# Earlier loads for W1 tiles in the steady blocks, and later sums of one W1 tile at the start, in a two-layer matmul with GELU

## The chip, the cores and the metric

The kernel runs on one core of one Trainium2 chip. The metric is the device time of one execution in microseconds (us), with the median of several executions quoted. A profiled execution also has a span, from its first to its last instruction, which is 1 to 2 us shorter than the time. The engines are called PE (TensorE), PEld (its weight loads), DVE (VectorE), ACT (ScalarE), POOL (GpSimd) and SP (SyncE, which here only issues DMA; SPq is its queue of instructions).

The Trainium skill, a set of notes on the chip, is cited by the title of the page and the section.

## The reference

```python
batch, m, k, h, n = 16, 512, 768, 3072, 768      # x, w1, b1, w2: normal draws, float32
y = np.matmul(x, w1) + b1
y = 0.5 * y * (1.0 + erf(y / np.sqrt(2.0)))
out = np.matmul(y, w2)
```

## The kernel before

The 8192 rows of x are worked in eight blocks of 1024. Both matmuls use a Strassen-like scheme: seven products of half-size operands in place of eight, paid for with sums and differences on DVE. W1 is cut into twelve tiles. A tile holds seven operands, made of its raw data by four sums on DVE (`prep_wt`), 672 KB in all in fp16. In the first two blocks, which are interleaved, each tile is loaded raw, gets its sums, and is stored in that form in device memory (`keep`). The six later blocks (the steady blocks) only read the stored tiles back (`load_wt`). In a steady block twelve units of the first matmul (`Unit1`, 4.53 us each) are followed by seven units of the second (`Unit3`).

PE runs the program of one unit (`i`) interleaved with the end of the unit before it (`j`). This is a cut from `period`; lines left out are marked with `...`, and the comments are mine:

```python
        def period(i, j, fill):
            ...
            if i:
                p1(i, 0, i.C)        # matmuls into bX
                copy_xy(i)           # ACT copies bX to bY
            ...
            if j:
                p7(j)                # matmuls into bY, then on DVE: c22 = bY + w
            fill(1)                  # sums on DVE, loads: fill(1) to fill(6)
            ...                      # p5(i): matmuls into bW, ACT copies them to w
            if j:
                p3(j)                # matmuls into bZ, then on DVE: c12 = bZ + w
            fill(3)
            if i:
                p6(i)                # matmuls into the bY that copy_xy filled
            if j:
                j.right_done()       # ACT: GELU of c12 and c22
            fill(4)
            if j:
                p4(j)                # matmuls into the bY that c22 was read from
            fill(5)
            if i:
                p2(i)
            fill(6)
```

`p6(i)` waits for ACT's `copy_xy(i)`. `p4(j)` adds to the same bank of bY from which DVE reads for c22, so it waits for that DVE add.

The homes of the tiles in steady blocks, and when they are asked for:

```python
    wt_late = [wt_at(o_wt2), wt_at(o_wt2 + WT_N)] + wt_own[:2]     # four homes
    ...
        def load_wt(n):
            hi = hi_of(n)
            if n >= NH:
                wts[n] = wt_late[n % 4]
                nc.sync.dma_start(out=wts[n], in_=w1s[hi][:])
                return
    ...
        def fill_mm1(sb, k, slot):
            ...
            if slot == 5:
                if k + 3 < NH and n + 3 not in wts:
                    load_wt(n + 3)
```

With four homes, tile k+3 goes where tile k-1 was, so SP waits until unit k-1 is finished. The next block's x tiles (POOL) and their transposes (SP) and the first ten W2 pieces (the "ring", SP) are asked for in the same units.

## Time and profile before

| | before |
|---|---|
| time, median of 6 runs | 854.43 us (853.19 to 855.50) |
| span of the profiled execution | 852.4 us |
| PE, DVE, ACT busy | 99%, 78%, 49% |
| start-to-start spacing of matmuls with 512, 384, 192 columns (medians) | 216, 162, 82 ns |
| all matmuls at their median spacing | 839.6 us |
| excess over that spacing, whole program | 7.8 us |

The spacing is the distance between the starts of successive matmuls in the timeline. "Excess" is the sum of what goes beyond the median spacing of the shape, and a "wait" of PE below is such an excess at one place. It is a little longer than the idle time that the profile prints in brackets, because the profile's matmul durations overlap.

From the page of the kernel before: busy time by engine, the chain of work that ended last by engine, and one group of matmuls (count, busy us, mean ns, idle us before them and what ended it):

```profile
PE 845.8 (99%) x6432; PEld 569.2 (67%) x6432; DVE 667.8 (78%) x1128; ACT 421.1 (49%) x686; POOL 83.3 (10%) x135
...
PE 93%; DMA 5%; ACT 1%; DVE 0%; issue 0%; POOL 0%; ACTq 0%
...
L383 PE MATMUL bX<-arena 128*128 128x512 f16 x564 | 138.6, 379 | 0.6 <-DMA arena<-w1s 0.5
```

The waits of PE, before (total us, times, longest us); those of L735 and bT lie in the first 14 us:

```profile
PE bX L735 <- DVE arena L721: 1.2, 1, 1.2
PE bX L383 <- DMA arena<-w1s: 0.5, 1, 0.5
PE bT L308 <- ACT arena L310: 0.4, 1, 0.4
PE bY L383 <- ACT bY L601: 0.4, 1, 0.4
PE bT L308 <- DVE arena L741: 0.2, 1, 0.2
```

Busy time says little about how full PE is ("Perfetto Trace Analysis", Identifying the Most-Contended Engine: matmuls are pipelined). The spacing says more. "TensorE: Matmul & The Clock Gate" (Wait — 56ns, not 53.3ns?) gives 215.7 ns for 512 columns at full clock, and this trace has 216. So PE is at its roof nearly everywhere, and a change of loads and sums can only win what stands in the few waits. Two places have waits that the change could touch.

The first is the second steady block. The chain of waits (start us, length us) names, apart from three x loads that are issued in the first 14 us, two loads in the whole program: one of a W1 tile at the start and one of a stored tile. The third line, from the timeline of PE, is the first use of that stored tile:

```profile
24.64 11.81 DMA arena<-in_w_dram
...
366.35 10.18 DMA arena<-w1s
```

```profile
376.58 0.82 PE L383 MATMUL bX<-arena 128*128 128x512 f16 x3 [0.55 <-DMA arena<-w1s]
```

Tile 10 was asked for at 366.35 us, landed at 376.53, and PE stood for 0.71 us.

The second place is at the start. This is the timeline of the kernel before from 33.8 to 48 us (start us, length us, engine, line, operation, tiles, in brackets the idle time before it and what ended it):

```profile
33.76 1.79 DVE L189 TENSOR_TENSOR arena<-arena 128x384 f16<-128x384 f16 x5
...
35.47 0.68 DVE L608 TENSOR_TENSOR arena<-bY,arena 128x512 f32<-128x512 f32 x1
...
36.47 1.14 DVE L189 TENSOR_TENSOR arena<-arena 128x384 f16<-128x384 f16 x3 [0.32 <-DMA arena<-in_w_dram]
37.53 0.68 DVE L636 TENSOR_TENSOR arena<-bZ,arena 128x512 f32<-128x512 f32 x1
...
38.24 1.15 ACT L399 ACTIVATE arena<-arena,b1t 128x1024 f16<-128x1024 f32 x1 [1.12 <-DVE arena L636]
...
41.13 0.60 ACT L601 COPY bY<-bX 128x512 f32<-128x512 f32 x1
...
41.78 1.46 PE L383 MATMUL bY<-arena 128*128 128x512 f16 x6 [0.38 <-ACT bY L601]
...
44.24 1.02 DVE L189 TENSOR_TENSOR arena<-arena 128x768 f16<-128x768 f16 x2
...
45.30 0.69 DVE L608 TENSOR_TENSOR arena<-bY,arena 128x512 f32<-128x512 f32 x1
...
46.40 1.46 PE L383 MATMUL bY<-arena 128*128 128x512 f16 x6
```

Read it downwards. Four of the five sums at 33.76 belong to W1 tile 1. The sums of tile 6 at 36.47 waited for the load of tile 6, which landed at 36.44. Behind them on DVE stands the c12 add (L636), behind that ACT's GELU (L399) and four more ACT operations without a pause, the last of them the copy that PE needs at 41.78. The c22 add (L608) ends at 45.99, and the second three of the six matmuls at 46.40 are p4, which needs it.

### The profile page before, as it was taken

Reading aid. Unit: us, or ns where it says so; the run is one execution under the profiler, and the core shown is the slowest. Engines: PE = TensorE matmul, PEld = TensorE weight load, DVE = VectorE, ACT = ScalarE, POOL = GpSimd, SP = SyncE. Lnnn points to the kernel's source line nnn. Section 1 sums busy time; section 2 is a strip of 40 time slices with the busy share of each in tenths; the row PEclk is TensorE's granted clock in tenths of the full one; section 3 lists DMA queues with packets and bytes.
Section 4 is the critical chain, followed back from the end, with each engine's and each line's share of the span. In section 5 each row is a group of like instructions: output and inputs, shape, how many; then the busy total and the mean of one; then the engine's idle time right before and its main releaser. Section 6 shows DMA issues by size and latency. Waiting matters only on the chain.

```text
span 852.4 us, 16481 instructions
## 1 busy us (share of the span) xinstructions
PE 845.8 (99%) x6432; PEld 569.2 (67%) x6432; DVE 667.8 (78%) x1128; ACT 421.1 (49%) x686; POOL 83.3 (10%) x135
## 2 busy tenths in 40 slices
PE   9999999999999999999999999999999999999998
PEld 5444445687544897448974499645995469944798
DVE  4956678786657998679976799667996689956998
ACT  4777762122277513774138722477216771267611
POOL 5021100002100002000020000200012000010000
PEclk9999999999999999999999999999999999999999
DMA  9995987649989698996989789896998969967398
GB/s 225 201 271 86 256 166 257 253 190 221 227 242 290 206 326 289 294 265 228 337 285 298 220 279 335 278 300 192 312 343 257 311 177 329 354 218 270 99 310 284
DMA packets 143522, 219.05 MB, mean 257 GB/s; under 512 B 61756, under 2 KB 84724, under 8 KB 143444
## 3 DMA queue, kind: packets, MB, share of 16 engines
q1 hardware_dynamic: 117968, 179.83, 66.0%
q0 software_dynamic: 25440, 38.15, 20.9%
q8 instruction: 50, 0.82, 0.4%
q14 instruction: 28, 0.23, 0.1%
q10 hardware_dynamic: 36, 0.01, 0.0%
HBM read 180.30 MB, written 47.87 MB: 268 GB/s over the span
## 4 chain that ended last, share of the span: by engine, by line
PE 93%; DMA 5%; ACT 1%; DVE 0%; issue 0%; POOL 0%; ACTq 0%
PE bY L383 20%; PE bY L488 15%; PE bX L383 13%; PE bX L488 10%; PE bZ L383 7%; PE bW L383 7%; PE bZ L488 5%; PE bW L488 5%; PE bY L427 5%; DMA arena<-in_x_dram 3%; PE bZ L427 2%; PE bW L427 2%; PE bX L427 2%; DMA arena<-in_w_dram 1%; DMA arena<-w1s 1%; PE bY L575 1%
## 5 line engine op out<-in xcount | busy, mean ns | idle before, releaser
L189 DVE TENSOR_TENSOR arena<-arena 128x1536 f16<-128x1536 f16 (+7 forms) x632 | 403.5, 669 | 6.0 <-PE bW L427 1.1
L383 PEld LDWEIGHTS <-arena 128*128 128x128 f16 x1974 | 192.4, 98 | 225.7 <-DMA arena<-w1s 1.8
L488 PEld LDWEIGHTS <-arena 128*128 128x128 f16 x3528 | 292.1, 98 | 8.4 <-issue 0.4
L383 PE MATMUL bY<-arena 128*128 128x512 f16 x846 | 214.4, 379 | 0.4 <-ACT bY L601 0.4
L608 DVE TENSOR_TENSOR arena<-bY,arena 128x512 f32<-128x512 f32 (+1 forms) x102 | 69.4, 681 | 126.7 <-PE bY L383 88.2
L383 PE MATMUL bX<-arena 128*128 128x512 f16 x564 | 138.6, 379 | 0.6 <-DMA arena<-w1s 0.5
L488 PE MATMUL bY<-arena 128*128 128x192 f16 x1500 | 138.3, 246 | 0.0
L601 ACT COPY bY<-bX 128x512 f32<-128x512 f32 (+1 forms) x143 | 78.6, 550 | 119.4 <-DVE arena L537 82.0
L399 ACT ACTIVATE arena<-arena,b1t 128x1024 f16<-128x1024 f32 x94 | 108.0, 1149 | 54.0 <-DVE arena L636 54.0
L621 ACT COPY arena<-bW 128x512 f32<-128x512 f32 (+1 forms) x147 | 81.0, 551 | 92.0 <-PE bW L488 43.9
L488 PE MATMUL bX<-arena 128*128 128x192 f16 x1020 | 93.1, 246 | 0.1
L636 DVE TENSOR_TENSOR arena<-bZ,arena 128x512 f32<-128x512 f32 (+1 forms) x102 | 69.3, 679 | 22.7 <-PE bZ L383 18.7
L383 PE MATMUL bZ<-arena 128*128 128x512 f16 x282 | 76.2, 379 | 0.0
L383 PE MATMUL bW<-arena 128*128 128x512 f16 x282 | 76.2, 379 | 0.0
L427 PEld LDWEIGHTS <-arena 128*128 128x128 f16 x528 | 51.6, 98 | 34.1 <-issue 0.2
L404 ACT ACTIVATE arena<-bX,b1t 128x512 f16<-128x512 f32 x94 | 64.0, 681 | 10.0 <-PE bX L383 10.0
L520 POOL DMA_DIRECT2D out_dram<-arena x42 | 30.5, 728 | 391.8 <-DVE arena L632 355.6
L404 ACT ACTIVATE arena<-bY,b1t 128x512 f16<-128x512 f32 x94 | 63.3, 674 | 0.0
L652 ACT COPY bZ<-bY 128x512 f32<-128x512 f32 (+1 forms) x54 | 29.0, 537 | 66.0 <-DVE arena L636 31.8
L294 POOL DMA_DIRECT2D arena<-in_x_dram x60 | 32.3, 544 | 265.0 <-DMA arena<-arena 154.6
L488 PE MATMUL bZ<-arena 128*128 128x192 f16 x504 | 48.5, 246 | 0.0
L488 PE MATMUL bW<-arena 128*128 128x192 f16 x504 | 48.5, 246 | 0.0
(60 smaller groups left out, 401.2 us busy)
## 6 DMA issues: line engine op xcount, KB each, us to landing
arena<-w2s SPq DMA_DIRECT2D x294, 288.0 KB, 4.6
arena<-w1s SPq DMA_DIRECT2D x72, 672.0 KB, 6.5
out_dram<-arena POOLq DMA_DIRECT2D x42, 384.0 KB, 4.7
w2s<-arena SPq DMA_DIRECT2D x49, 288.0 KB, 3.9
arena<-in_x_dram POOLq DMA_DIRECT2D x60, 192.0 KB, 6.8
w1s<-arena SPq DMA_DIRECT2D x12, 672.0 KB, 7.8
arena<-in_w_dram POOLq DMA_DIRECT2D x17, 384.0 KB, 7.2
out_dram<-arena SPq DMA_DIRECT2D x17, 384.0 KB, 3.5
```

What stands on the lines that cost most here:

```text
L189: nc.vector.tensor_tensor(out=o, in0=a, in1=b, op=op)
L294: nc.gpsimd.dma_start(out=xhs[t], in_=xr[:, sb * 8 + t, :])
L383: nc.tensor.matmul(out=dst[:, 0:RH], lhsT=w1_op(self.wt, slot)[:, c, :], rhs=a[:, c, :], start=first and c == 0, stop=c == self.C - 1, ski ...
L399: nc.scalar.activation(out=self.G[1][:, hi, :, :], in_=self.tmp, func=GELU, bias=b1t[:, 2 * hi + 1:2 * hi + 2])
L404: nc.scalar.activation(out=self.G[0][:, hi, row, :], in_=bank[:, 0:RH], func=GELU, bias=b1t[:, 2 * hi:2 * hi + 1])
L427: nc.tensor.matmul(out=dst[:, 0:N2], lhsT=a, rhs=w[:, :, c, :], start=first and c == 0, stop=c == self.C - 1, skip_group_check=True)
L488: nc.tensor.matmul(out=dst[:, t * N4:(t + 1) * N4], lhsT=a, rhs=w[:, c, :], start=first and c == 0 and t == ts[0], stop=c == NQ - 1, skip_ ...
L520: eng.dma_start(out=orr[:, s0:s0 + 2, right * N2:(right + 1) * N2], in_=self.dst[:, r].rearrange("p t h n -> p t (h n)"))
L601: nc.scalar.copy(out=bY[u.g % 2][:, 0:u.F], in_=bX[u.g % 2][:, 0:u.F])
L608: nc.vector.tensor_tensor(out=u.c22(), in0=bY[u.g % 2][:, 0:u.F], in1=w[:, 0:u.F], op=ADD)
L621: nc.scalar.copy(out=w[:, 0:u.F], in_=bW[:, 0:u.F])
L636: nc.vector.tensor_tensor(out=u.c12(), in0=bZ[:, 0:u.F], in1=w[:, 0:u.F], op=ADD)
```

## The change

Its intent, as far as the edit shows it: at the start, ask for the four sums of tile 1 two units later, and for the stores of the tiles in another order, with tile 1 behind tiles 2 to 6; in the steady blocks, give tiles 4, 5 and 6 homes of their own in the room of nested sums that are made only later, and ask for tiles 3 to 10 in the first five units.

```diff
+    wt_far = [wt_at(o_lev + 8 * RH + k * WT_N) for k in range(3)]
+    assert 8 * RH + 3 * WT_N <= 8 * LB
@@ load_wt
-                wts[n] = wt_late[n % 4]
+                sb, k = divmod(n, NH)
+                wts[n] = wt_far[k - 4] if 4 <= k < 7 else wt_late[(sb + 2 + k - 7 * (k > 6)) % 4]
@@ fill_a (the start), slot 4 and slot 5
-                if pos in (3, 4):
-                    prep_wt(pos - 3)
+                if pos in (3, 6):
+                    prep_wt(pos // 6)
...
-                if seq[pos][0] == 1:
-                    keep(seq[pos][1])
+                for n in {at[1, 0]: (0, 2, 3, 4, 6, 5), at[1, 1]: (1,)}.get(
+                        pos, seq[pos][1:] if pos > at[1, 6] and seq[pos][0] and seq[pos][1] > 6 else ()):
+                    keep(n)
@@ fill_mm1 (steady blocks), slot 5
-                if k + 3 < NH and n + 3 not in wts:
-                    load_wt(n + 3)
+                for m in {0: (3, 4), 1: (5, 6, 7), 2: (8,), 3: (9,), 4: (10,), 8: (11,)}.get(k, ()):
+                    if sb * NH + m not in wts:
+                        load_wt(sb * NH + m)
```

The added lines shift the line numbers: L383 becomes L386, L601 L604, L608 L611, L636 L639.

## The prediction

> **What bounds the kernel.** TensorE. The page shows PE busy 845.8 of 852.4 us (99%), DVE 78%, ACT 49%. Since the Trainium skill ("Perfetto Trace Analysis", Identifying the Most-Contended Engine) warns that matmul occupancy says little about the distance to the roof, I took the spacing of matmul starts in the timeline: 216 ns for 512 columns, 162 for 384, 82 for 192. "TensorE: Matmul & The Clock Gate" (Wait — 56ns, not 53.3ns?) states 215.7 ns for 512: the trace agrees, TensorE streams at full rate. All matmuls at these spacings make 839.6 us; 7.8 are excess. The change touches two places of it:
>
> - 41.78 us: 0.55, and 46.40: 0.08. PE waits for ACT's copy into bY.
> - 376.6 to 388.4 us, second steady block: 0.71 + 0.18 + 0.25 = 1.14. W1 tile 10, asked for at 366.35, landed at 376.53 (10.2 us; median 6.5), tile 11 at 381.25, each just late. In the chain of waits the other blocks repeat every 102.9 us, this one takes 104.1; 12 x 21 x 0.216 + 7 x 84 x 0.0825 = 102.9, so the others have nothing left.
>
> At most 1.8 us (0.2%) can be won.
>
> **What the change does.** Nothing is added or removed.
>
> (a) Steady blocks: tiles 4, 5, 6 get homes of their own. Tiles 7 to 10 are asked for three units (14 us) earlier. Between 353 and 367 us four W1 loads of 672 KB shrink to one, where x loads, transposes and ring loads share the DMA engines (one set for all issuers, skill "DMA: Bandwidth & Descriptors", Issuing engines are not separate DMA queues). Tile 11 keeps its place but meets less traffic. I expect all 1.14 us back, and no new wait from the early burst (tiles 4 to 6 near 330 us, used 10 us later or more).
>
> (b) Start: the four sums of tile 1 (0.39 us each) leave 34.0 to 35.6 us and come at about 45.2. This does not remove the 0.55 us: the next sums on DVE wait for tile 6's load, landed 36.44, which nothing moves (DVE already idled 0.32 us there). After it the DVE add at 37.5, the GELU at 38.24 and four more ACT operations in a row up to the copy ending 41.73 stay. But at 45.2 the sums' 1.5 us stand ahead of the bY add (L608), which then ends at about 47.3 instead of 45.99; the p4 matmuls into that bY started at 47.05. Estimate: 0.3 us of new wait. The stores' new order costs nothing: tile 1's store lands by about 54 us, the load over it is asked for at 55.9.
>
> **Sum.** 854.24 − 1.14 + 0.3 = 853.4 us; range 852.0 to 854.8. Faster by over 2%: 0.01; within 2%: 0.98; slower by over 2%: 0.01.
>
> **What would show it.** (a): no PE wait on w1s in the waits; steady blocks all near 102.9 us; landing of w1s under 10 us. (b): the gap near 41.8 us stays about 0.5 us, and one of about 0.3 appears before a bY matmul near 47, released by DVE L611 (the old L608).
>
> **What would make it wrong.** The stall at 376 us differs between executions, so the median holds less of it; tile 6 lands earlier, and (b) wins 0.5 instead; the early burst delays the first x loads, their transposes hold up SyncE's queue, and tile 11 is late in every block (5 x 0.5 us lost).

## The result, and the profile after

| | before | after |
|---|---|---|
| time, median of 6 runs | 854.43 us (853.19 to 855.50) | 853.25 us (853.03 to 854.13) |
| span of the profiled execution | 852.4 us | 851.5 us |

The ratio is 0.9988 with a 95% interval of 0.9975 to 1.0001. A ratio is the mean time of one kernel's fast runs over that of the other's of the same rounds, so it is not quite the ratio of the medians quoted. 853.25 lies in the range of 852.0 to 854.8. The interval just includes 1, so the times alone do not show a gain; what follows about tenths of a microsecond rests on the profiles.

The waits of PE, after. The wait on stored tiles is gone from the list (those of L738 and bT lie in the first 14 us):

```profile
PE bX L738 <- DVE arena L724: 1.2, 1, 1.2
PE bT L311 <- DVE arena L744: 1.2, 2, 0.9
PE bY L386 <- ACT bY L604: 0.2, 1, 0.2
```

The same stretch of the start, after:

```profile
33.81 0.35 DVE L191 TENSOR_TENSOR arena<-arena 128x384 f16<-128x384 f16 x1
...
35.06 0.69 DVE L611 TENSOR_TENSOR arena<-bY,arena 128x512 f32<-128x512 f32 x1 [0.91 <-PE bY L386]
...
36.31 1.14 DVE L191 TENSOR_TENSOR arena<-arena 128x384 f16<-128x384 f16 x3 [0.55 <-DMA arena<-in_w_dram]
...
41.63 1.46 PE L386 MATMUL bY<-arena 128*128 128x512 f16 x6 [0.17 <-ACT bY L604]
...
44.08 2.46 DVE L191 TENSOR_TENSOR arena<-arena 128x768 f16<-128x768 f16 x6
...
46.24 1.76 PE L386 MATMUL bY<-arena 128*128 128x512 f16 x6
46.46 0.68 DVE L611 TENSOR_TENSOR arena<-bY,arena 128x512 f32<-128x512 f32 x1
```

The sums of tile 1 are gone from 33.8 us, and DVE only waits longer (0.91 and 0.55 us in place of 0.32) for what it waited for before. At 44.08 six sums stand where two stood, and the c22 add (L611) ends at 47.14 in place of 45.99. The six matmuls at 46.24 take 1.76 us in place of 1.46 at the same place before: the second three of them are p4, and they waited 0.31 us for that add. The profile's own chain of waits after the change shows it (start us, length us):

```profile
46.46 0.69 DVE arena L611
47.15 0.04 issue
47.19 0.81 PE bY L386 x3
```

Traffic in the second steady block (stretch and its length in us; busy us of PE, PEld, DVE, ACT and POOL, each with its count of instructions; clock; mean busy share of the DMA engines; GB/s). The share counts each packet in full in the stretch in which it starts, so it can exceed 1. Before:

```profile
323.00:338.00 15.00, 15.00 (x143) 12.02 (x141) 13.30 (x21) 3.94 (x7) 3.63 (x5) 1.00 0.83 302
338.00:353.00 15.00, 15.00 (x72) 6.72 (x70) 8.07 (x13) 11.77 (x18) 2.92 (x5) 1.00 0.96 267
353.00:367.00 14.00, 14.00 (x66) 6.36 (x65) 10.10 (x17) 10.89 (x18) 1.06 (x2) 1.00 1.16 291
367.00:382.00 15.00, 14.44 (x67) 6.25 (x66) 9.77 (x18) 11.76 (x19) 1.06 (x2) 1.00 1.11 268
```

After:

```profile
323.00:338.00 15.00, 15.00 (x145) 12.13 (x143) 13.29 (x21) 3.89 (x7) 3.63 (x5) 1.00 0.98 365
338.00:353.00 15.00, 15.00 (x72) 6.74 (x70) 8.11 (x13) 11.61 (x19) 2.85 (x5) 1.00 1.08 314
353.00:367.00 14.00, 14.00 (x66) 6.34 (x65) 10.19 (x18) 10.89 (x18) 1.66 (x4) 1.00 1.12 312
367.00:382.00 15.00, 15.00 (x71) 6.86 (x70) 10.44 (x20) 12.41 (x20) 0.53 (x1) 1.00 0.76 158
```

The bytes moved forward, from the last stretch to the three before it. PE is busy for all of the last stretch now (15.00 in place of 14.44).

Where the time went, as differences of PE's excess between the two profiles:

| place | before | after | difference |
|---|---|---|---|
| 370 to 384 us: stored tiles late, second steady block | 0.90 | 0.00 | -0.90 |
| 580 to 600 us: end of the first matmul in the fourth steady block | 0.16 | 0.06 | -0.10 |
| 384 to 390 us: see the shifting run below | 0.25 | 0.26 | 0 |
| near 41.7 us: ACT's copy late | 0.55 | 0.34 | -0.21 |
| near 47.2 us: c22 add late | 0 | 0.31 | +0.31 |

The sum is -0.90 us, and the spans differ by 0.9 us. (The first 14 us, which the change does not touch, had 0.1 us more excess after.)

### The profile page after: what moved, and what is told of

It is laid out like the page before. It is cut to its first block, busy times and chain, and to the rows that moved or that the text cites. A ratio compares the mean times of both kernels' runs of the same rounds, so it can differ in the third digit from the quotient of the medians.

```text
span 851.5 us, 16488 instructions
## 1 busy us (share of the span) xinstructions
PE 844.9 (99%) x6432; PEld 568.8 (67%) x6432; DVE 667.0 (78%) x1128; ACT 420.9 (49%) x686; POOL 83.3 (10%) x135
## 4 chain that ended last, share of the span: by engine, by line
PE 94%; DMA 4%; DVE 1%; ACT 0%; issue 0%; POOL 0%; DVEq 0%; ACTq 0%
PE bY L386 20%; PE bY L491 15%; PE bX L386 13%; PE bX L491 10%; PE bW L386 7%; PE bZ L386 7%; PE bZ L491 5%; PE bW L491 5%; PE bY L430 5%; DMA arena<-in_x_dram 3%; PE bZ L430 2%; PE bX L430 2%; PE bW L430 2%; DMA arena<-in_w_dram 1%; PE bY L578 1%; DVE arena L191 1%
## 5 line engine op out<-in xcount | busy, mean ns | idle before, releaser
L386 PEld LDWEIGHTS <-arena 128*128 128x128 f16 x1974 | 192.5, 98 | 224.7 <-issue 1.1
L386 PE MATMUL bY<-arena 128*128 128x512 f16 x846 | 214.5, 379 | 0.3 <-ACT bY L604 0.2
L611 DVE TENSOR_TENSOR arena<-bY,arena 128x512 f32<-128x512 f32 (+1 forms) x102 | 69.3, 680 | 126.3 <-PE bY L386 87.6
L386 PE MATMUL bX<-arena 128*128 128x512 f16 x564 | 138.2, 379 | 0.0
L604 ACT COPY bY<-bX 128x512 f32<-128x512 f32 (+1 forms) x143 | 78.6, 550 | 119.3 <-DVE arena L540 81.9
L639 DVE TENSOR_TENSOR arena<-bZ,arena 128x512 f32<-128x512 f32 (+1 forms) x102 | 69.2, 679 | 20.7 <-PE bZ L386 17.9
L386 PE MATMUL bZ<-arena 128*128 128x512 f16 x282 | 76.2, 379 | 0.0
L386 PE MATMUL bW<-arena 128*128 128x512 f16 x282 | 76.2, 379 | 0.0
L655 ACT COPY bZ<-bY 128x512 f32<-128x512 f32 (+1 forms) x54 | 29.0, 537 | 65.9 <-DVE arena L639 33.7
```

The source lines that it names most:

```text
L386: nc.tensor.matmul(out=dst[:, 0:RH], lhsT=w1_op(self.wt, slot)[:, c, :], rhs=a[:, c, :], start=first and c == 0, stop=c == self.C - 1, ski ...
L604: nc.scalar.copy(out=bY[u.g % 2][:, 0:u.F], in_=bX[u.g % 2][:, 0:u.F])
L611: nc.vector.tensor_tensor(out=u.c22(), in0=bY[u.g % 2][:, 0:u.F], in1=w[:, 0:u.F], op=ADD)
L639: nc.vector.tensor_tensor(out=u.c12(), in0=bZ[:, 0:u.F], in1=w[:, 0:u.F], op=ADD)
```

## The experiments

My theory: the early asks in the steady blocks win about 0.9 us or more. The start wins nothing and costs 0.3 us near 47 us. The wait near 41.7 us hangs on the landing of tile 6. The rival: relieving DVE at the start is what helps, and the wait near 41.7 us is ACT's or DVE's own load. The experiments ran in three batches of four kernels, and each batch has its own runs of the kernel before; the second batch ran on another chip than the first and the third. Times of different batches should not be compared to a few tenths of a microsecond. At that size I read the profiles. Even these differ by chance: the first 14 us, whose work no edit here changes, had between 3.2 and 4.4 us of PE's excess in the fourteen profiles. All kernels gave correct results.

### The kernel before once more (e0)

No edit.

> The kernel before, unchanged, profiled once more: does its wait at 376 us come in every execution? If it does: waits of 0.7 and 0.2 us (each within 0.2) at 376 and 381 us, and 0.25 at 388. If it is chance: under 0.3 us in all at 376 and 381.

Measured: one run, 854.38 us, at a clock of 1.0. From the timeline of PE:

```profile
376.49 0.82 PE L383 MATMUL bX<-arena 128*128 128x512 f16 x3 [0.80 <-DMA arena<-w1s]
...
587.84 0.82 PE L383 MATMUL bX<-arena 128*128 128x512 f16 x3 [0.18 <-DMA arena<-w1s]
```

The waits at 376 and 381 us were 0.96 and 0.22 us, so the first is a little over the stated 0.7 with its margin of 0.2, and the one at 388 us was 0.25. Tile 10 took 10.44 us to land. At 580 to 600 us there were 0.52 us, of which 0.06 near 599 us come in the changed kernel too and are no W1 wait (see the shifting run). So the late tiles come in every profile of the old loads that I have (three with the start-only run), and they cost 0.9 to 1.2 us in the second steady block and, where the 0.06 us is left out, 0.1 to 0.46 us in the fourth.

### The steady half alone (e1) and the start alone (e2)

e1 is the changed kernel with the two edits of `fill_a` undone. e2 is the kernel before with only those two edits.

```diff
-                if pos in (3, 6):
-                    prep_wt(pos // 6)
+                if pos in (3, 4):
+                    prep_wt(pos - 3)
...                               # and keep(seq[pos][1]) as before
```

> The changed kernel with its start put back (sums of tile 1 at the old place, stores in the old order); the steady blocks stay changed. My theory (the steady half wins, the start costs 0.3 us at 47 us and leaves the wait at 41.7 us alone): no wait near 47.2 us (0.31 in the changed kernel), a wait of 0.35 to 0.6 us near 41.7 us, none at 376 to 381 us, 0.25 at 387.7; time 0.2 to 0.4 us below the changed kernel, about 852.9 to 853.1. Rival (moving the sums relieves DVE and is what shrank the wait at 41.7 us from 0.55 to 0.34): the wait at 41.7 is back at 0.55 and the time is level with the changed kernel within 0.15 us.

> The kernel before with only the start changed (sums and stores of tile 1 later). My theory: a new wait of about 0.3 us near 47 us, the wait near 41.7 us stays at 0.3 to 0.6 us in step with the landing of tile 6, the waits at 376 and 381 us (0.71 + 0.18) stay; time 0.1 to 0.4 us above the kernel before. Rival (the start is the half that wins): 0.5 us or more below the kernel before.

Measured, in one batch with the kernel before at 854.36 us:

| | time, median | ratio to before | near 41.7 | near 47.2 | 370 to 384 |
|---|---|---|---|---|---|
| e1, steady only | 852.90 us (852.59 to 853.75) | 0.9985 [0.9973, 0.9998] | 0.15 | none | 0 |
| e2, start only | 854.35 us (853.43 to 856.48) | 1.0005 [0.9992, 1.0017] | 0.42 | 0.31 | 1.11 |

The start alone brings exactly the new wait near 47 us and leaves the late tiles. It is not faster than before. The steady half alone has the gain and no wait near 47 us. Its wait near 41.7 us was smaller than in the changed kernel, although the sums of tile 1 were back at their old place. That is outside the numbers of both theories (0.35 to 0.6, or 0.55), and the runs below explain it.

### What sets the wait near 41.7 us (e4)

The load of W1 tile 6 is issued one place earlier:

```diff
-                load_next_x(1, (2, 6, 3, 7))
-                load_wt(6)
+                load_next_x(1, (2, 6, 3))
+                load_wt(6)
+                load_next_x(1, (7,))
```

> The changed kernel with the load of W1 tile 6 issued ahead of the last x tile instead of behind it. My theory (the wait near 41.6 us starts with DVE waiting for the landing of tile 6 at 36.28, which holds the add, the GELU and the chain of ACT operations behind it): tile 6 lands near 35.4 us, the DVE gap of 0.55 us before its sums is gone or under 0.1, the wait of 0.34 us near 41.6 is gone, and the wait near 47.2 shrinks below 0.1 because DVE runs 0.5 us earlier; time 0.4 to 0.7 us below the changed kernel, about 852.6 to 852.9. Rival (the wait near 41.6 us is ACT's own work, five operations in a row, whatever the landing): it stays at 0.3 us, time level.

Measured: 853.17 us (852.20 to 853.50), ratio 0.9982 [0.9969, 0.9996]. Tile 6 landed at 35.18 us, DVE did not pause before its sums, the wait near 41.7 us was gone, and the one near 47.2 us shrank to 0.09. So the waits went as my theory said. The time did not follow fully: in this profile the excess of the first 14 us was 4.38 us against 3.67 in the changed kernel's, so part of what it saved here had been lost earlier. This one profile also has its matmuls due later (41.99 us), so it is not clean proof by itself. The profile of e7, below, has the same edit and matmuls due as early as in the kernel before: tile 6 landed at 35.28, and they started at 41.24 without a wait.

The proof is in all the profiles together. The matmuls near 41.7 us start a fixed time after tile 6 lands, whenever DVE stood idle for that tile:

| run | tile 6 landed | matmuls would have been due | they started | start minus landing | wait |
|---|---|---|---|---|---|
| before | 36.44 | 41.24 | 41.78 | 5.34 | 0.55 |
| after | 36.28 | 41.29 | 41.63 | 5.35 | 0.34 |
| e2, start only | 36.12 | 41.04 | 41.47 | 5.35 | 0.42 |
| e3, below | 36.45 | 41.02 | 41.79 | 5.34 | 0.78 |
| e6, below | 36.24 | 41.48 | 41.58 | 5.34 | 0.10 |
| e8, below | 36.38 | 41.55 | 41.72 | 5.34 | 0.18 |
| after, again (e9) | 36.87 | 41.43 | 42.21 | 5.34 | 0.78 |

("Due" is the start minus the wait. e5 and e11, below, gave 5.35 and 5.34 with waits of 0.71 and 0.75.) The wait is therefore a race between a load and the arrays, and it fell between 0.10 and 0.78 us from execution to execution. In the two profiles where DVE was still busy with tile 1's sums when tile 6 landed (e0 and e1, landing at 35.98 and 36.06), start minus landing was 5.48 and 5.46. Moving the sums of tile 1 can thus win at most some 0.15 us, and only when tile 6 lands early.

The new wait near 47.2 us ends with the same load. In the changed kernel and in e2, e5, e6, e8 and e11 the p4 matmuls started 10.91 to 10.92 us after tile 6 landed, whatever the wait near 41.7 us had been (0.10 to 0.75): with tile 1's sums ahead of it, DVE's row of work from that landing to the c22 add is the later one there.

### The sums of tile 1 behind the add (e3)

```diff
-                if pos in (3, 6):
-                    prep_wt(pos // 6)
+                if pos == 3:
+                    prep_wt(0)
             if slot == 1:
+                if pos == at[1, 0]:
+                    prep_wt(1)
```

> The changed kernel with the four sums of tile 1 asked for one unit later still, behind the add into c22 (L611 of the changed kernel) instead of ahead of it. My theory (the wait near 47.2 us is the p4 matmuls waiting for that add behind 1.5 us of sums): that wait, 0.31 us, is gone, nothing new appears, the wait near 41.6 us stays at 0.3 to 0.5; time 0.3 us below the changed kernel, about 852.95. Rival (it is the total work of DVE in these units, wherever the sums stand): a wait of 0.2 us or more appears somewhere between 47 and 52 us, time level with the changed kernel.

Measured: 852.97 us (852.57 to 853.36), ratio 0.9984 [0.9971, 0.9996]. The timelines of DVE and PE in this run:

```profile
36.47 1.15 DVE L191 TENSOR_TENSOR arena<-arena 128x384 f16<-128x384 f16 x3 [1.11 <-DMA arena<-in_w_dram]
...
41.79 1.46 PE L386 MATMUL bY<-arena 128*128 128x512 f16 x6 [0.62 <-ACT bY L604]
...
45.31 0.69 DVE L611 TENSOR_TENSOR arena<-bY,arena 128x512 f32<-128x512 f32 x1
45.91 1.14 DVE L191 TENSOR_TENSOR arena<-arena 128x384 f16<-128x384 f16 x3
...
46.41 1.46 PE L386 MATMUL bY<-arena 128*128 128x512 f16 x6
```

The add is back at 45.31, three of tile 1's sums follow it, and the six matmuls take 1.46 us again: the wait near 47.2 us is gone and nothing replaced it up to 52 us. The same sums cost 0.31 us ahead of the add and nothing just behind it, so it is the order and not the amount of DVE work. The wait near 41.8 us was 0.78 us here, in step with its landing, and larger than the 0.3 to 0.5 that I had stated.

### Homes without early asks (e5 and e11), tile 10 alone late (e6)

```diff
-                for m in {0: (3, 4), 1: (5, 6, 7), 2: (8,), 3: (9,), 4: (10,), 8: (11,)}.get(k, ()):
+                for m in {k: (k + 3,) for k in range(9)}.get(k, ()):                                   # e5, e11
+                for m in {0: (3, 4), 1: (5, 6, 7), 2: (8,), 3: (9,), 7: (10,), 8: (11,)}.get(k, ()):  # e6
```

> The changed kernel with the new homes but the old times of asking (tile k + 3 in unit k). My theory (the homes alone win nothing, the early asking does): tile 10 asked for near 366 us lands in about 10 us in the second steady block, a wait of 0.5 to 0.9 us in all at 376 to 381 us is back, time 0.6 to 1.1 us above the changed kernel, about 854.0 to 854.3. Rival (the homes themselves take the waits away): no wait on W1 tiles, time level with the changed kernel.

> The changed kernel with tile 10 alone asked for at its old time (unit 7), tiles 4 to 9 early. Theory A (what matters is that tile 10 is asked for early): asked for near 366 us with 10.2 us until use, it lands late again or just in time in 9 to 10 us, with a wait of up to 0.7 us. Theory B (what matters is that the other early loads have left the stretch 353 to 367 us, so that the DMA engines are freer): it lands in 5 to 7.5 us, no wait, time level with the changed kernel within 0.15 us. I hold B.

> The kernel with the new homes and the old times of asking (tile k + 3 in unit k) once more; its first profile showed no wait at 376 us, against my expectation, with tile 10 landing only some 0.6 us before its use, yet it was 0.56 us slower than its neighbour of the same call. If the early asks matter as I said, some executions are late: a wait of over 0.1 us at 376 to 384 us or in a later block, time 0.2 us or more above the changed kernel of this call. If the homes alone do it: no such wait again and level within 0.15 us.

| second steady block | tile 10 asked for | landed | took | wait at 370 to 384 | time, median |
|---|---|---|---|---|---|
| before | 366.35 | 376.53 | 10.18 | 0.90 | 854.43 us |
| after | 352.95 | 358.58 | 5.63 | 0 | 853.25 us |
| e5, homes only | 365.71 | 375.37 | 9.67 | 0 | 853.72 us (853.21 to 854.21) |
| e11, the same again | 362.29 | 371.53 | 9.24 | 0 | 853.31 us (853.04 to 854.07) |
| e6, only 10 late | 363.84 | 369.49 | 5.66 | 0 | 853.16 us (853.05 to 853.47) |

Here my theory fell in part. I had expected that homes without early asks would bring the waits back, and neither profile shows one. The homes let SP issue tiles 4 and 5 at 326.8 and 330.6 us even in e5, because they no longer wait for units 0 and 1 to end. (The times in the table are from different batches.) But tile 10 lands only 0.6 us before its first use at 375.98 in e5, and 4.4 us in e11, against 17 us in the changed kernel. In e6 the old time of asking for tile 10 is harmless: with the other tiles out of the way it takes 5.66 us. So the homes alone removed the wait in what was profiled, and the early asks buy margin. Early asks without the homes were not run. In its batch e5 was 0.56 us slower than e6 by median (854.82 for the kernel before), in the third batch e11 was 0.25 us slower than the changed kernel. Whether late tiles in some executions caused that is open, because both profiles had none and the ranges of e11 and the changed kernel overlap.

### Shifting ACT's stream (e8)

The wait of 0.25 us near 387.7 us, which I had counted to the late tiles, stayed in the changed kernel. There an ACT copy (L655) starts at 384.45 us although the DVE and PE instructions that it waits for had ended by 384.1, and the ACT operations behind it are late by as much. The edit puts twelve tiny copies into ACT's stream one block earlier, where ACT idles:

```diff
+            if sb == ONE and k == 3 and slot == 4:
+                for _ in range(12):
+                    nc.scalar.copy(out=pad[:, 0:1], in_=b1t[:, 0:1])
```

> The changed kernel with twelve tiny copies put into ACT's stream in the matmul phase of the first steady block, where ACT idles; they shift the place of all later ACT instructions by twelve or more. It tests the wait of 0.25 us near 387.7 us that the change did not remove although I had counted it to the W1 tiles: there an ACT copy starts 0.32 us after both its releases, in both kernels at the same instruction. Theory C (it hangs on the place of the instruction in ACT's stream): the late start moves to another instruction and the wait near 387.7 is under 0.1 us. Theory D (it hangs on what happens around it in the second block, DMA or the operations ahead of it): it stays at 0.25 us. Time within 0.3 us of the changed kernel either way.

Measured: 852.87 us (852.50 to 853.11), ratio 0.9976 [0.9961, 0.9991]. The timelines of ACT and PE of the changed kernel:

```profile
384.45 0.57 ACT L655 COPY bZ<-bY 128x512 f32<-128x512 f32 x1 [1.12 <-DVE arena L639]
...
387.67 1.15 PE L491 MATMUL bX<-arena 128*128 128x192 f16 x12
```

and of the shifted one, where the program is the same but for the twelve copies:

```profile
384.19 0.57 ACT L656 COPY bZ<-bY 128x512 f32<-128x512 f32 x1 [0.84 <-DVE arena L640]
...
387.44 1.15 PE L492 MATMUL bX<-arena 128*128 128x192 f16 x12
```

The copy now starts 0.05 us after its last release, the wait of PE is under 0.01 us, and the 0.06 us near 598 us are gone too. So this wait hangs on where the instruction stands in ACT's stream, not on W1.

The count of ACT's instructions in the traces supports this. In all twelve profiles without the copies, the ACT instructions that idle and then start over 0.13 us after the semaphore they waited for are, apart from one at 1.4 us, the 448th, the 704th and the 960th of ACT's instructions in the trace (those of its sequencer counted too): 256 apart, and 0.36, 0.19 and 0.37 us late in the changed kernel (at 384.45, 597.69 and 819.66 us). In the two profiles with the copies there is none, so the lateness did not move to another instruction, as Theory C had it; PE only has new waits of 0.07 us near 406 and 612 us. What delays these three stays open.

### The changed kernel again (e9), both mends (e7), and both with the shift (e10)

e7 joins the edits of e3 and e4, e10 joins those of e3, e4 and e8.

> The changed kernel, unchanged, once more, on the same chip as the next three, as their measure and for a second profile. Expected: no wait at 370 to 384 us, 0.25 near 387.7, 0.3 near 47.2, and a wait near 41.6 us equal to the landing of tile 6 minus the time the matmuls are due plus 5.34 us (the sum that held within 0.02 us in every earlier profile in which DVE stood idle before tile 6's sums); time 853.0 to 853.5.

> The changed kernel with both mends of the start: sums of tile 1 behind the c22 add, tile 6 loaded ahead of the last x tile. Expected: no wait over 0.1 us near 41.6 or near 47.2, none at 370 to 384, 0.25 near 387.7 stays; 0.5 to 0.8 us below the changed kernel of this call, about 852.5. Rival (the start of the program is paced by the loads of the first 12 us, whatever follows): level within 0.2 us.

> The last kernel and the twelve tiny ACT copies of the shifting run. Expected if the lateness near 387.7 us hangs on the place in ACT's stream: that wait under 0.1 us, 0.2 to 0.3 us below the last kernel, about 852.3, the fastest of all. Otherwise 0.25 stays and the times are level.

In one batch with the kernel before at 853.87 us:

| | time, median | mean of the five | ratio to before |
|---|---|---|---|
| e9, changed kernel again | 853.06 us (853.03 to 854.15) | 853.34 us | 0.9989 [0.9976, 1.0001] |
| e7, both mends | 853.06 us (852.80 to 853.57) | 853.09 us | 0.9986 [0.9973, 0.9998] |
| e10, both mends and shift | 852.89 us (852.20 to 853.20) | 852.84 us | 0.9983 [0.9970, 0.9995] |

The profile of e9 was of its execution of 854.15 us: tile 6 landed at 36.87, and the waits between 39 and 46 us were 0.38, 0.78 and 0.35 us. That is what a slower execution of the changed kernel looks like. Near 47 us the changed kernel's 0.31 us came back (at 48.12 here).

e7 missed its expected 852.5. The wait near 41.7 us and that near 47.2 us were gone, but a new one of 0.43 us stood at 44.26 us. From the timelines of DVE and PE of e7:

```profile
41.65 1.15 DVE L191 TENSOR_TENSOR arena<-arena 128x768 f16<-128x768 f16 x2 [0.64 <-DMA arena<-arena]
...
44.26 0.81 PE L386 MATMUL bY<-arena 128*128 128x512 f16 x3 [0.27 <-DVE bZ L657]
```

The next sums on DVE, those of x, wait for the last transpose of x, which landed at 41.56 us. The edit itself put the load of that x tile one place later, but this is little of it: the transpose was issued at 36.68 us against 36.55 in the changed kernel, and in e9, without the edit, it landed at 42.00. Taking one load out of the way only uncovered the next. This supports the rival of that run, that the loads of the start set the pace. Its wait near 387.7 us stayed, and e10 removed it as expected; e10 kept a 0.42 us wait at 44.5. e10 is the fastest by median of its batch, but it missed its expected 852.3, and its 0.17 us against e9 are not settled by five runs each.

## Why the prediction was right

- The time was forecast at 853.4 us and measured at 853.25. By ratio the gain is 0.12%, forecast 0.10% (854.24 to 853.4). The number alone is a weak test: the range also holds the median of the kernel before (854.43). What bears the prediction out is the waits.
- "At most 1.8 us can be won" held for the change, because PE's waits that it touches hold no more. The one version that gained more against the kernel before of its batch (e8, 1.95 us by median) also removes the wait that hangs on ACT's stream.
- (a), steady blocks: the waits at 376 and 381 us vanished, as stated (0.90 us). Two sizes were off. Of the 1.14 us that I booked, the 0.25 near 388 us was no W1 wait, as e8 showed. And "the others have nothing left" was wrong by 0.10 us in this profile and 0.46 in e0, in the fourth block. The two errors have opposite signs. The landing of stored tiles was to stay "under 10 us" and its longest was 10.3 (asked for at 636 us), in the early burst, where it hurt nobody.
- The reason that I gave for (a) was half right. I put the relief in 353 to 367 us, but there the DMA share only fell from 1.16 to 1.12, and it fell from 1.11 to 0.76 after 367 us. The traffic of other loads moved up into the space. That transfers of all issuers share one set of DMA engines ("DMA: Bandwidth & Descriptors", Issuing engines are not separate DMA queues) fits it: the same 672 KB took 10.2 us in the crowd and 5.7 us without it (e6). What moved away in e6 were SP's own loads; that POOL's transfers slow SP's, no run here shows.
- (b), the start: the new wait near 47 us was estimated at 0.3 us and measured at 0.31, from the same four sums, released by the add on L611. e3 shows the order as the cause. The wait near 41.7 us stayed, for the reason given. Its size, "about 0.5 us", was a size of one execution: it was 0.34 us after, and 0.10 to 0.78 in other runs. So it is in part luck that the change in PE's waits came as close to the forecast (-0.90 us against -0.84): 0.21 us of it is this race, which the change does not set. "Which nothing moves" was too strong, since the landing of tile 6 varied between 36.0 and 36.9 us where no edit touched its load.

## What to carry to other kernels

When the busiest engine is at its roof, list its waits with their releasers before estimating a change, because the change can win no more than those it touches. Moving work off a queue helps only if that work was what the queue waited for: here DVE was waiting for a load, and the same sums set down ahead of an add with a close deadline made a new wait, while one place further back they were free. A wait that is a race with a load should be measured in several executions before it is called a cost.

## What the Trainium skill lacked or had wrong

- No page has a delay at a fixed place in an engine's stream with its size: here the 448th, 704th and 960th ACT instructions of the trace started 0.18 to 0.37 us after the semaphore they waited for, and none started so late once twelve tiny instructions were put in earlier (e8, e10). It would belong to "Runtime: NRT & Kernel Launch" (Instruction fetch mechanics), which tells of refills in blocks of 256 instructions but gives no duration for crossing from one to the next. Whether the two have to do with each other, no run here shows.
- "DMA: Bandwidth & Descriptors" (Bandwidth) gives durations for transfers by size, 6.15 us for 1 MB, measured as the engines' busy span. It has no figure there for a transfer among others: here loads and stores of the same 672 KB took from 3.0 to 11.7 us from issue to landing in these profiles, which decided whether PE waited.
- Nothing that these runs test was found wrong. The spacing of matmuls in "TensorE: Matmul & The Clock Gate" (Wait — 56ns, not 53.3ns?), 215.7 ns, agreed with the trace (216 ns).
